# An expert mixture on one Trainium2 core: the split experts' weights in 1024-wide chunks, and one more weight buffer

## The chip, the cores and the metric

The kernel runs on one core of one Trainium2 chip. Times are device microseconds (us) of that core, from the start of an execution to its end; lower is better. TensorE (PE in the profile) does the matrix products, VectorE (DVE) and ScalarE (ACT) work on tiles, GpSimd (POOL) does little here, and SyncE (SP) issues nearly all loads from memory in one queue. Two changes are told apart when they differ by more than about half a per cent.

## The reference

Two decoder layers over 256 tokens of width 1024, all in f32. Each layer has modulation from a conditioning vector, a normalisation, a mixer (banded attention beside a state-space scan) and a channel mixer. The channel mixer of the first layer is a dense gated network; that of the second is a mixture of eight experts of hidden width 3584, of which each token uses its two best. The change is in that mixture:

```
logits = hf @ router_w
top_val, top_idx = lax.top_k(logits, 2)          # of 8 experts
gates = softmax(top_val)
# for each expert e, on the tokens that chose it:
y = (silu(xb @ w_gate[e]) * (xb @ w_up[e])) @ w_down[e]     # 1024 -> 3584 -> 1024
out[token] += gate * y
```

The weights of all eight experts are read, whatever the tokens choose: 352 MB of the 466 MB that the kernel reads.

## The kernel before

**Units and buffers.** All large weights come through one class, `Stream` (L60 to L235). It cuts them into *units* of 1 MB (128 partitions of 2048 f32) in the order in which the program uses them. `pump` (called whenever a unit is released) issues the next units on SP's queue as long as a buffer is to be had. There are eight *raw* buffers, handed out in turn, and some tiles of other stages that are *lent* to the stream when those stages are over; the trace calls them raw and slot. SP issues loads strictly in order: a load whose buffer is not yet free holds up every load behind it. The buffer that a load takes is settled when the program is built, and the loads in flight or held are at most as many as there are buffers: in the mixture the stream is 11 units ahead of its use, and 12 in its first expert.

**Two kinds of experts.** The eight experts are sorted by the number of their tokens and take places 0 to 7, which are of kinds H, L, H, L, H, L, H, L. An H expert (up to 128 tokens) works with each weight and each token value split in two parts, `hi` and `lo`: ScalarE copies half a unit to `hi` (L156) and VectorE subtracts it from the unit to get `lo` (L157), 128x1024 at a time. Five such half units fit in their pool. `mm3` (L682 to L684) then makes three matmuls for one product. A unit of an H expert is free again when both its halves have been split. An L expert (up to 64 tokens) is not split: TensorE reads the unit itself as f32 (gate and up at L1507, down at L1529), and the unit is free when its last matmul is done. An expert has 42 units: 14 each of gate, up and down.

**Chunks.** The hidden width is worked off in chunks: 512 columns wide in H experts (7 chunks, each 2 units of gate, 2 of up and 2 of down; a row of a gate or up unit is 2 KB), 1024 wide in L experts (3 such chunks and one of 512; a row is 4 KB). For each chunk the program makes gate and up, then `sg` = silu(gate) (L1636, ScalarE) times up (L1637, VectorE), and then, while the next chunk's gate and up run, turns `sg` over (`transp`, L1557 to L1559, or `transpl`, L1518 and L1552) and multiplies it with the down weights. The down units of a chunk thus stand behind the gate and up units of the next chunk, in the queue as well: the last two down units of an H expert come after the eight gate and up units of the first chunk of the L expert behind it.

**Around the experts.** Tokens are gathered by matmuls with one-hot matrices (`gather_part`, L1478, into `xh` and `xl`), for two places at a time, some of it between other matmuls (`parts`, `pend`). `combine` scales an expert's result (`yh`, L1578) and adds it to the tokens. Ahead of place 4 stands `overflow` (L1225 to L1300), a branch on the number of tokens beyond the places' capacity (L1230); with this data the number is zero and the body is not run, but each engine tests the number, and SP lets its loads land first. The body has loads of its own, `ow` (L1264, on SP's queue).

The lines that the prediction speaks of are `load` (L123) and `_split` (L156, L157) of the stream:

```
self.nc.sync.dma_start(dst, src)
...
self.last_hi = nc.scalar.activation(hi[:, o:o + w], t, AF.Copy).ins
self.last_lo = nc.vector.tensor_tensor(lo[:, o:o + w], t, hi[:, o:o + w].bitcast(F32), op=OP.subtract).ins
```

## Time and profile before

| What | Value |
|---|---|
| median of 3 runs | 1438.55 us (1433.37 to 1441.64) |
| the profiled execution | 1443.44 us, its span 1441.3 us |
| TensorE busy | 1340.4 us (93%) |
| VectorE busy | 862.2 us (60%) |
| ScalarE busy | 652.8 us (45%) |
| moved by DMA | 468.78 MB, mean 325 GB/s |
| mean granted TensorE clock | 0.970 of full speed |

The span is the time from the first to the last instruction of the profiled execution; the rest of its 1443.44 us lies around it. The mixture of experts takes from about 504 to 1427 us of the span. A mean rate over the span mixes stages with different limits, so the mixture is read from stretches of it.

### The profile page before, as it was taken

The numbers are of one execution on the slowest core, as the hardware profiler recorded it, in microseconds if no ns is written. First come the engines' busy times: TensorE is split into PE (matmuls) and PEld (weight loads), VectorE is DVE, ScalarE is ACT, GpSimd is POOL, SyncE is SP. The second block draws the span as 40 slices with busy tenths as digits, with TensorE's granted clock in tenths as the row PEclk, the third lists the DMA queues.
The fourth block names the chain that finished last, engine by engine and source line by source line (L and its number), as shares of the span: only waits on it lengthen the run. The fifth ranks groups of instructions, "written<-read, shape, count | busy, mean of one in ns | idle before, by whom it ended". The sixth has DMA issues, their size and how long they took to land. (4 is left out here: it accounts for less than half of the span.)

```text
span 1441.3 us, 20237 instructions
## 1 busy us (share of the span) xinstructions
PE 1340.4 (93%) x7642; PEld 964.4 (67%) x7642; DVE 862.2 (60%) x1299; ACT 652.8 (45%) x925; POOL 20.1 (1%) x22
## 2 busy tenths in 40 slices
PE   5999999999899899999889999969999979999985
PEld 3788699999798678864367873337885336785431
DVE  5587598777688589941068862038983116884202
ACT  3456444444456467731057742036772015773001
POOL 0020000000010000000000000000000000000000
PEclk9999999999999999999989999989999999999998
DMA  9963899999335369979999979999998999995995
GB/s 314 331 237 118 282 388 357 331 332 330 127 132 176 117 243 371 349 265 410 399 393 395 396 309 399 402 391 347 395 402 347 409 396 395 393 398 227 375 403 228
DMA packets 181478, 468.78 MB, mean 325 GB/s; under 512 B 10528, under 2 KB 39424, under 8 KB 178304
## 3 DMA queue, kind: packets, MB, share of 16 engines
q1 hardware_dynamic: 178880, 466.72, 86.3%
q8 instruction: 62, 1.02, 0.3%
q10 hardware_dynamic: 2496, 0.72, 0.2%
q14 instruction: 40, 0.33, 0.1%
HBM read 466.36 MB, written 1.05 MB: 324 GB/s over the span
## 5 line engine op out<-in xcount | busy, mean ns | idle before, releaser
L157 DVE TENSOR_TENSOR lo<-raw,hi 128x1024 fp32r<-128x1024 f32 (+1 forms) x372 | 447.0, 1226 | 138.5 <-ACT hi L156 133.9
L156 ACT ACTIVATE hi<-raw 128x1024 fp32r<-128x1024 f32 (+1 forms) x372 | 385.8, 1058 | 250.5 <-PE ps_m L683 69.3
L682 PE MATMUL ps_w<-hi,xh 128*128 128x512 f32 x448 | 183.9, 410 | 12.6 <-ACTq L1230 8.1
L683 PE MATMUL ps_w<-lo,xh 128*128 128x512 f32 x448 | 183.0, 409 | 3.4 <-DVE lo L157 3.4
L684 PE MATMUL ps_w<-hi,xh 128*128 128x512 f32 x448 | 182.0, 406 | 2.4 <-issue 2.3
L1637 DVE TENSOR_TENSOR sg<-sg,ps_w 128x512 f32<-128x512 f32 (+1 forms) x44 | 29.0, 660 | 222.0 <-PE ps_w L1507 170.6
L1507 PE MATMUL ps_w<-raw,xl 128*64 128x512 f32 (+1 forms) x688 | 143.9, 547 | 9.1 <-DMA raw<-in_moe_w_up 7.3
L682 PE MATMUL ps_m<-act_hi,hi 128*128 128x256 f32 (+1 forms) x368 | 104.6, 285 | 7.6 <-ACT hi L156 4.7
L682 PEld LDWEIGHTS ps_w<-hi,xh 128*128 128x128 f32 x448 | 87.2, 195 | 36.2 <-ACTq L1230 9.0
L1507 PEld LDWEIGHTS ps_w<-raw,xl 128*64 128x64 f32 x688 | 48.4, 136 | 85.9 <-issue 68.8
L683 PEld LDWEIGHTS ps_w<-lo,xh 128*128 128x128 f32 x448 | 87.0, 194 | 27.8 <-DVE lo L157 7.2
L683 PE MATMUL ps_m<-act_lo,hi 128*128 128x256 f32 (+1 forms) x368 | 104.3, 284 | 0.1
L684 PE MATMUL ps_m<-act_hi,lo 128*128 128x256 f32 (+1 forms) x368 | 104.0, 284 | 0.4 <-DVE lo L157 0.4
L157 DVE TENSOR_TENSOR lo<-slot,hi 128x1024 fp32r<-128x1024 f32 (+1 forms) x88 | 97.9, 1147 | 10.7 <-ACT hi L156 10.0
L684 PEld LDWEIGHTS ps_w<-hi,xh 128*128 128x128 f32 x448 | 86.8, 194 | 23.4 <-issue 3.0
L1636 ACT ACTIVATE sg<-ps_w 128x512 f32<-128x512 f32 (+1 forms) x44 | 25.3, 576 | 162.5 <-PE ps_w L1507 139.0
L156 ACT ACTIVATE hi<-slot 128x1024 fp32r<-128x1024 f32 (+1 forms) x88 | 86.3, 1000 | 25.1 <-PE ps_w L684 15.5
L1529 PE MATMUL ps_d<-raw,ht 128*64 128x512 f32 x344 | 81.0, 600 | 9.3 <-DMA raw<-in_moe_w_down 9.3
L682 PEld LDWEIGHTS ps_m<-act_hi,hi 128*128 128x128 f32 (+1 forms) x368 | 68.2, 185 | 11.5 <-ACT hi L156 5.2
L1507 PE MATMUL ps_w<-slot,xl 128*64 128x512 f32 (+1 forms) x336 | 70.9, 535 | 1.6 <-DMA slot<-in_moe_w_up 1.6
L684 PEld LDWEIGHTS ps_m<-act_hi,lo 128*128 128x128 f32 (+1 forms) x368 | 68.2, 186 | 2.8 <-issue 1.7
L683 PEld LDWEIGHTS ps_m<-act_lo,hi 128*128 128x128 f32 (+1 forms) x368 | 68.3, 186 | 0.7 <-DVE act_lo L677 0.3
(410 smaller groups left out, 2221.1 us busy)
## 6 DMA issues: line engine op xcount, KB each, us to landing
raw<-in_moe_w_down SPq DMA_DIRECT2D x87, 1024.0 KB, 14.0
raw<-in_moe_w_up SPq DMA_DIRECT2D x84, 1024.0 KB, 13.6
raw<-in_moe_w_gate SPq DMA_DIRECT2D x75, 1024.0 KB, 14.7
raw<-in_ada_w SPq DMA_DIRECT2D x40, 1024.0 KB, 6.8
slot<-in_moe_w_gate SPq DMA_DIRECT2D x46, 512.0 KB, 13.7
slot<-in_moe_w_up SPq DMA_DIRECT2D x40, 512.0 KB, 12.6
slot<-in_moe_w_down SPq DMA_DIRECT2D x30, 512.0 KB, 13.0
raw<-in_w_in SPq DMA_DIRECT2D x14, 1024.0 KB, 8.4
```

The costliest lines, as they stand in the source:

```text
L156: self.last_hi = nc.scalar.activation(hi[:, o:o + w], t, AF.Copy).ins
L157: self.last_lo = nc.vector.tensor_tensor(lo[:, o:o + w], t, hi[:, o:o + w].bitcast(F32), op=OP.subtract).ins
L682: PE.matmul(o_, s_hi, m_hi, start=start, stop=False, skip_group_check=True)
L683: PE.matmul(o_, s_hi, m_lo, start=False, stop=False, skip_group_check=True)
L684: PE.matmul(o_, s_lo, m_hi, start=False, stop=stop, skip_group_check=True)
L1507: PE.matmul(b[half * c_:half * (c_ + 1), 0:wide], xl[:, kk_, 0:half], S.col(j, o_, o_ + wide), start=(kk_ == 0), stop=(kk_ == KT - 1), ski ...
L1529: PE.matmul(y[half * c_:half * (c_ + 1), :], ht[:, ft % nm, ft // nm, :], S.col(j, t_ * D + c_ * 512, t_ * D + (c_ + 1) * 512), start=(ch ...
L1636: A.activation(sg[:, 0:wide], g[:, 0:wide], AF.Silu)
L1637: V.tensor_tensor(sg[:, 0:wide], sg[:, 0:wide], u[:, 0:wide], op=OP.mult)
```

## The change

H experts are worked off in the same chunks as L experts: three of 1024 columns and one of 512. A gate or up unit of a wide chunk then holds two row blocks of 1024 columns (a row is 4 KB) where it held four of 512, and each is multiplied into two result banks (gate: two of the pool `w`; up: one of `w` and one of `m`). `transp` and `sg` are done twice per chunk, on both halves. The gathered tokens of an L expert, `xl`, are kept only for the 64 columns in use, in the tile `masks` that held two attention masks; so the tile `act_lo`, which held `xl`, is lent to the stream as one more buffer of 1 MB for the whole mixture. The loads `ow` of the branch's body are issued on ScalarE's queue. Lines move by 2 to 14.

```diff
-    chunks = {"H": [(c0, 512) for c0 in range(0, ED, 512)], "L": [(c0, min(1024, ED - c0)) for c0 in range(0, ED, 1024)]}
+    chunks = [(c0, min(1024, ED - c0)) for c0 in range(0, ED, 1024)]
+    LAST = len(chunks) - 1
 
...
     def add_down(p, ch):
-        c0, width = chunks[kinds[p]][ch]
+        c0, width = chunks[ch]
         for r0 in range(c0, c0 + width, 2 * P):
             add_m("d", moe_w_down, p, r0, 2 * P, 0, D)
 
     first_moe = len(units)
     pend_d = None
     for p in range(NE):
-        for ch, (c0, width) in enumerate(chunks[kinds[p]]):
+        for ch, (c0, width) in enumerate(chunks):
             rows = 2048 // width * P
             for wt, tag in ((moe_w_gate, "g"), (moe_w_up, "u")):
                 for r0 in range(0, D, rows):
...
-    amask2 = const.tile([P, 2, T], BF)
-    amask4 = const.tile([P, 4, P], BF)
+    masks = act.tile([P, 2, 2 * T], BF, name="masks", tag="masks")
+    amask2 = masks[:, 0].rearrange("p (a t) -> p a t", a=2)
+    amask4 = masks[:, 1].rearrange("p (a t) -> p a t", a=4)
...
-            nc.sync.dma_start(t, w[0, bass.ds(e, 1), r0:r0 + P, c0:c0 + 512].rearrange("e p f -> p (e f)"))
+            nc.scalar.dma_start(t, w[0, bass.ds(e, 1), r0:r0 + P, c0:c0 + 512].rearrange("e p f -> p (e f)"))
...
-        xl = act.tile([P, KT, P], F32, name="xl", tag="act_lo")
+        xl = act.tile([P, KT, half], F32, name="xl", tag="masks")
 
...
+        S.lend(len(units), lambda: [act.tile([P, 2 * D], F32, name="slot", tag="act_lo")])
...
-        def proj(tag, e, b, parts=()):
+        def proj(tag, p, banks, parts=()):
             parts = list(parts)
-            for kh in range(2):
-                w = S.take((tag, e), 4)
-                for k in range(4):
-                    kk_ = kh * 4 + k
-                    if parts and k % 2 == 0:
+            nb = len(banks)
+            nk = 4 // nb
+            for kh in range(KT // nk):
+                w = S.take((tag, p), nk)
+                for k in range(nk):
+                    kk_ = kh * nk + k
+                    if parts and kk_ % 2 == 0:
                         parts.pop(0)()
-                    mm3(b, xh[:, 0, kk_, :], xh[:, 1, kk_, :], w.hi(k), w.lo(k), kk_ == 0, kk_ == KT - 1)
-                    if k % 2:
+                    for n, b in enumerate(banks):
+                        cols = (n * 512, (n + 1) * 512)
+                        mm3(b, xh[:, 0, kk_, :], xh[:, 1, kk_, :], w.hi(k, *cols), w.lo(k, *cols), kk_ == 0, kk_ == KT - 1)
+                    if nb == 2 or k % 2:
                         S.used()
             while parts:
                 parts.pop(0)()
             step_pend()
 
-        def transp(sg):
-            p_ = ps("m")
-            for j in range(4):
-                PE.transpose(p_[:, j * P:(j + 1) * P], sg[:, j * P:(j + 1) * P], ident)
-            hh = act.tile([P, 4, P], F32R, name="hh", tag="mt", bufs=2)
-            hl = act.tile([P, 4, P], F32R, name="hl", tag="pt", bufs=2)
-            pv = p_.rearrange("p (j s) -> p j s", j=4)
-            with tc.issue_after(S.last_hi):
-                A.activation(hh, pv, AF.Copy)
-            with tc.issue_after(S.last_lo):
-                V.tensor_tensor(hl, pv, hh.bitcast(F32), op=OP.subtract)
-            return hh, hl
-
-        def down(e, ch, y, hh, hl):
-            for hf in range(2):
-                w = S.take(("d", e), 2)
+        def transp(sgs):
+            out_ = []
+            for sg in sgs:
+                p_ = ps("m")
+                for j in range(4):
+                    PE.transpose(p_[:, j * P:(j + 1) * P], sg[:, j * P:(j + 1) * P], ident)
+                hh = act.tile([P, 4, P], F32R, name="hh", tag="mt", bufs=2)
+                hl = act.tile([P, 4, P], F32R, name="hl", tag="pt", bufs=2)
+                pv = p_.rearrange("p (j s) -> p j s", j=4)
+                with tc.issue_after(S.last_hi):
+                    A.activation(hh, pv, AF.Copy)
+                with tc.issue_after(S.last_lo):
+                    V.tensor_tensor(hl, pv, hh.bitcast(F32), op=OP.subtract)
+                out_.append((hh, hl))
+            return out_
+
+        def down(p, ch, y, hs):
+            for u in range(chunks[ch][1] // 256):
+                w = S.take(("d", p), 2)
                 for k in range(2):
+                    ft = u * 2 + k
+                    hh, hl = hs[ft // 4]
                     for n_ in range(2):
-                        j = hf * 2 + k
-                        mm3(y[n_], hh[:, j, :], hl[:, j, :], w.hi(k, n_ * 512, (n_ + 1) * 512),
-                            w.lo(k, n_ * 512, (n_ + 1) * 512), ch == 0 and j == 0, ch == 6 and j == 3)
+                        mm3(y[n_], hh[:, ft % 4, :], hl[:, ft % 4, :], w.hi(k, n_ * 512, (n_ + 1) * 512),
+                            w.lo(k, n_ * 512, (n_ + 1) * 512), ch == 0 and ft == 0, chunks[ch][0] + (ft + 1) * P == ED)
                     S.used()
 
...
+                nb = width // 512 if kind == "H" else 1
+                g = [ps("w") for _ in range(nb)]
                 if kind == "H":
                     proj("g", p, g, parts)
                 else:
-                    projl("g", p, width, g)
+                    projl("g", p, width, g[0])
                 parts = ()
                 if prev is not None:
                     step = flip(prev)
-                u = ps("w")
+                u = [ps(t) for t in ("w", "m")[:nb]]
                 if kind == "H":
                     proj("u", p, u)
                 else:
-                    projl("u", p, width, u)
...
-                sg = act.tile([P, 512], F32, name="sg", tag="rm", bufs=2)
-                A.activation(sg[:, 0:wide], g[:, 0:wide], AF.Silu)
-                V.tensor_tensor(sg[:, 0:wide], sg[:, 0:wide], u[:, 0:wide], op=OP.mult)
-                if ch == last and kind == "L" and p + 1 < NE:
+                sg = []
+                for g_, u_ in zip(g, u):
+                    s_ = act.tile([P, 512], F32, name="sg", tag="rm", bufs=2)
+                    A.activation(s_[:, 0:wide], g_[:, 0:wide], AF.Silu)
+                    V.tensor_tensor(s_[:, 0:wide], s_[:, 0:wide], u_[:, 0:wide], op=OP.mult)
+                    sg.append(s_)
+                if ch == LAST and kind == "L" and p + 1 < NE:
                     S.prime()
```

The order of instructions shows what this moves at three places. The first is SP's queue where expert 6 (H) ends and expert 7 (L) begins: each row is one load, a name ending in a number is the buffer's tile, and in brackets are the semaphores that it waits for (DMAHW for a landing, DVE and PE for the release of the buffer by that engine). Before:

```order
L123 DMA slot_11822<-in_moe_w_down 128x2x1024 [waits DMAHW5_49,DVE_49]
...
L123 DMA raw_11844<-in_moe_w_down 128x2x1024 [waits DMAHW6_49,DVE_49]
...
L123 DMA raw_11872<-in_moe_w_gate 128x2x1024 [waits DMAHW7_49,DVE_49]
...
L123 DMA slot_11894<-in_moe_w_gate 128x2x1024 [waits DMAHW5_49,DMAHW0_49,DVE_49]
...
L123 DMA slot_11953<-in_moe_w_gate 128x1024 [waits DMAHW1_49,PE_49]
...
L123 DMA slot_11954<-in_moe_w_gate 128x1024 [waits DMAHW2_49,PE_49]
...
L123 DMA raw_11961<-in_moe_w_gate 128x2x1024 [waits DMAHW3_49,PE_49]
```

The changed kernel, the same loads:

```order
L123 DMA raw_11793<-in_moe_w_down 128x2x1024 [waits DMAHW1_49,DVE_49]
...
L123 DMA slot_11821<-in_moe_w_down 128x2x1024 [waits DMAHW2_49,DVE_49]
...
L123 DMA raw_11843<-in_moe_w_gate 128x2x1024 [waits DMAHW3_49,DVE_49]
...
L123 DMA slot_11865<-in_moe_w_gate 128x1024 [waits DMAHW4_49,DVE_49]
...
L123 DMA slot_11866<-in_moe_w_gate 128x1024 [waits DMAHW5_49,DVE_49]
...
L123 DMA raw_11889<-in_moe_w_gate 128x2x1024 [waits DMAHW6_49,PE_49]
...
L123 DMA raw_11948<-in_moe_w_gate 128x2x1024 [waits DMAHW7_49,PE_49]
```

The first two rows are the last down units of expert 6, which stand in the queue behind the eight gate and up units of expert 7's first chunk; behind them come the gate units of its second chunk. Of these the second (two loads where its buffer is a slot of two tiles) has moved: before, it takes the slot of the first row, and waits for that unit's landing (DMAHW5) and for VectorE, which splits it; now its slot was given back by VectorE earlier, and the first load that waits for expert 7 itself (PE) is the third gate unit.

The second place is SP's queue at the branch ahead of place 4 (`COMPARE_AND_BRANCH`, L1230, now L1232). Before:

```order
L123 DMA raw_8579<-in_moe_w_down 128x2x1024 [waits DMAHW4_49,PE_49]
...
L123 DMA raw_8589<-in_moe_w_down 128x2x1024 [waits DMAHW5_49,PE_49]
...
L123 DMA raw_8602<-in_moe_w_gate 128x4x512 [waits DMAHW6_49,PE_49]
...
L123 DMA raw_8608<-in_moe_w_gate 128x4x512 [waits DMAHW7_49,PE_49]
...
L123 DMA raw_8614<-in_moe_w_up 128x4x512 [waits DMAHW0_49,PE_49]
...
L123 DMA raw_8620<-in_moe_w_up 128x4x512 [waits DMAHW1_49,DVE_49]
L1230 COMPARE_AND_BRANCH
```

The changed kernel, up to the branch, and then the first loads behind the branch's body:

```order
L123 DMA raw_8503<-in_moe_w_down 128x2x1024 [waits DMAHW4_49,PE_49]
...
L123 DMA raw_8519<-in_moe_w_gate 128x2x1024 [waits DMAHW5_49,PE_49]
...
L123 DMA raw_8529<-in_moe_w_gate 128x2x1024 [waits DMAHW6_49,PE_49]
L1232 COMPARE_AND_BRANCH
...
L123 DMA raw_8544<-in_moe_w_gate 128x2x1024 [waits DMAHW7_49,PE_49]
...
L123 DMA slot_8554<-in_moe_w_gate 128x2x1024 [waits DMAHW0_49,PE_49]
...
L123 DMA raw_8572<-in_moe_w_up 128x2x1024 [waits DMAHW1_49,PE_49]
```

The branch has moved up by eight loads: it stood behind the last up unit of expert 4's second chunk, and it stands now behind that expert's second gate unit.

The third is TensorE where expert 4 (H) ends and expert 5 (L) begins; `oh` and `htok` are the one-hot matrix and the tokens of the gather, `ps_w` is a bank of gate or up. Before:

```order
L683 MATMUL ps_a<-lo,hh 128x512
L684 MATMUL ps_a<-hi,hl 128x512
L1478 MATMUL ps_m<-oh,htok_h 128x256 [waits PE_49]
L1478 MATMUL ps_m<-oh,htok_h 128x256 x3
L1478 MATMUL ps_m<-oh,htok_l 128x256 [waits PE_49]
L1478 MATMUL ps_m<-oh,htok_l 128x256 x3
L1478 MATMUL ps_m<-oh,htok_h 128x256 [waits PE_49]
L1478 MATMUL ps_m<-oh,htok_h 128x256 x3
L1478 MATMUL ps_m<-oh,htok_l 128x256 [waits PE_49,Activation_49]
L1478 MATMUL ps_m<-oh,htok_l 128x256 x3
L1507 MATMUL ps_w<-raw,xl 64x512 [waits DMAHW0_49,DVE_49]
```

The changed kernel, at the first matmuls of this gather:

```order
L684 MATMUL ps_w<-hi,xh 128x512 [waits Activation_49]
L1480 MATMUL ps_m<-oh,htok_l 128x256 [waits DVE_49,PE_49]
L1480 MATMUL ps_m<-oh,htok_l 128x256 x3
L1480 MATMUL ps_m<-oh,htok_h 128x256 [waits DVE_49,PE_49]
L1480 MATMUL ps_m<-oh,htok_h 128x256 x3
L685 MATMUL ps_w<-lo,xh 128x512 [waits DVE_49]
L686 MATMUL ps_w<-hi,xh 128x512
L684 MATMUL ps_w<-hi,xh 128x512
```

The gather stood in one piece between the last down matmuls of expert 4 and the first gate matmuls of expert 5 (L1507); it now stands between matmuls of expert 4's last gate and up.

## Rows read from the trace of the kernel before

**Rows 1.** The page: busy time by engine, and GB/s in 40 slices.

```profile
PE 1340.4 (93%) x7642; PEld 964.4 (67%) x7642; DVE 862.2 (60%) x1299; ACT 652.8 (45%) x925; POOL 20.1 (1%) x22
...
GB/s 314 331 237 118 282 388 357 331 332 330 127 132 176 117 243 371 349 265 410 399 393 395 396 309 399 402 391 347 395 402 347 409 396 395 393 398 227 375 403 228
```

**Rows 2.** Stretches inside an L expert, an H expert, an H expert's gate units.

```profile
core 0: us, PE busy (x) PEld busy (x) DVE busy (x) ACT busy (x) POOL busy (x), PEclk, DMA share, GB/s
880.00:920.00 40.00, 39.05 (x186) 15.63 (x187) 5.54 (x11) 3.66 (x6) 0.00 (x0) 1.00 1.03 409
1020.00:1040.00 20.00, 20.00 (x92) 16.23 (x91) 18.22 (x17) 16.10 (x18) 0.00 (x0) 1.00 1.04 392
785.00:787.50 2.50, 2.50 (x13) 2.01 (x12) 2.50 (x3) 1.55 (x2) 0.00 (x0) 1.00 1.05 387
```

**Rows 3.** The same view where experts pass from H to L, and the branch.

```profile
610.00:620.00 10.00, 10.00 (x47) 8.13 (x46) 8.97 (x9) 7.67 (x9) 0.00 (x0) 1.00 0.75 249
620.00:630.00 10.00, 10.00 (x56) 8.05 (x55) 3.27 (x8) 2.23 (x7) 0.00 (x0) 1.00 0.49 193
630.00:640.00 10.00, 10.00 (x51) 4.02 (x51) 6.68 (x13) 5.37 (x8) 0.00 (x0) 1.00 0.54 186
...
850.00:860.00 10.00, 10.00 (x54) 6.97 (x54) 5.15 (x12) 1.33 (x5) 0.00 (x0) 1.00 0.70 269
860.00:870.00 10.00, 10.00 (x46) 3.27 (x44) 0.00 (x0) 3.83 (x6) 0.00 (x0) 1.00 0.51 175
970.00:980.00 10.00, 10.00 (x44) 6.02 (x43) 6.85 (x7) 5.67 (x7) 0.00 (x0) 1.00 0.65 230
...
1090.00:1100.00 10.00, 10.00 (x50) 4.07 (x50) 1.66 (x5) 2.48 (x4) 0.00 (x0) 1.00 0.57 181
...
1310.00:1320.00 10.00, 10.00 (x59) 7.15 (x59) 3.08 (x6) 1.15 (x3) 0.00 (x0) 1.00 0.74 294
1320.00:1330.00 10.00, 10.00 (x50) 3.39 (x48) 0.00 (x0) 4.87 (x6) 0.00 (x0) 1.00 0.00 0
1330.00:1340.00 10.00, 7.44 (x22) 4.53 (x19) 5.82 (x6) 0.00 (x0) 0.00 (x0) 0.72 0.43 149
```

**Rows 4.** SP's timeline: start and length of issuing a few loads, waiting included.

```profile
620.52 14.79 SPq L123 DMA_DIRECT2D raw<-in_moe_w_gate  x3
...
852.73 11.46 SPq L123 DMA_DIRECT2D raw<-in_moe_w_gate  x2
...
1079.64 18.25 SPq L123 DMA_DIRECT2D raw<-in_moe_w_gate  x3
...
1311.77 0.37 SPq L123 DMA_DIRECT2D raw<-in_moe_w_gate  x1
1334.52 1.55 SPq L123 DMA_DIRECT2D slot<-in_moe_w_gate  x3
```

**Rows 5.** TensorE's timeline at the three later passages.

```profile
858.00 3.65 PE L1507 MATMUL ps_w<-slot,xl 128*64 128x512 f32 x14
...
861.84 1.94 PE L1507 MATMUL ps_w<-raw,xl 128*64 128x512 f32 x8
...
1084.05 0.63 PE L1478 MATMUL ps_m<-oh,htok_h 128*128 128x256 f32 x4
...
1316.72 1.94 PE L1507 MATMUL ps_w<-slot,xl 128*64 128x512 f32 x8
```

**Rows 6.** VectorE's timeline where expert 7 begins; in brackets idle before, releaser.

```profile
1331.53 0.69 DVE L1637 TENSOR_TENSOR sg<-sg,ps_w 128x512 f32<-128x512 f32 x1 [14.53 <-PE ps_w L1507]
1332.13 2.35 DVE L157 TENSOR_TENSOR lo<-slot,hi 128x1024 fp32r<-128x1024 f32 x2
1334.41 0.68 DVE L1559 TENSOR_TENSOR hl<-ps_m,hh 128x512 fp32r<-128x512 f32 x1
```

**Rows 7.** The branch on TensorE's queue: count, ns minimum, median, maximum.

```profile
L1230 PEldq COMPARE_BRANCH  x1: 6286/6286/6286, 948.6 to 948.6; - x1
```

**Rows 8.** ScalarE's timeline at expert 4's first landing.

```profile
950.66 2.00 ACT L156 ACTIVATE hi<-raw 128x1024 fp32r<-128x1024 f32 x2 [15.94 <-DMA raw<-in_moe_w_gate]
```

**Rows 9.** The chain that ended last: start, length, what, line.

```profile
1406.67 18.06 DMA raw<-in_moe_w_down
```

More of the change, by code (lines that the diff above doesn't have):

```diff
@@ L1482, in gather_part @@
                 if kinds[p] == "L":
-                    A.activation(xl[:, ks], banks[0][:, :, q], AF.Copy)
-                    V.tensor_tensor(xl[:, ks], banks[1][:, :, q], xl[:, ks], op=OP.add)
+                    A.activation(xl[:, ks], banks[0][:, :, q, 0:half], AF.Copy)
+                    V.tensor_tensor(xl[:, ks], banks[1][:, :, q, 0:half], xl[:, ks], op=OP.add)
                 else:
@@ L1506, in projl @@
                         o_ = k * width + c_ * wide
-                        PE.matmul(b[half * c_:half * (c_ + 1), 0:wide], xl[:, kk_, 0:half],
+                        PE.matmul(b[half * c_:half * (c_ + 1), 0:wide], xl[:, kk_, :],
                                   S.col(j, o_, o_ + wide), start=(kk_ == 0), stop=(kk_ == KT - 1), skip_group_check=True)
@@ L1521, in downl @@
         def downl(p, ch, y, ht):
-            c0, width = chunks["L"][ch]
+            c0, width = chunks[ch]
             nm = width // 2 // P
@@ L1599, in flip @@
             if kinds[p] == "H":
-                hh, hl = transp(sg_)
-                return lambda y: down(p, ch, y, hh, hl)
-            ht = transpl(sg_, chunks["L"][ch][1])
+                hs = transp(sg_)
+                return lambda y: down(p, ch, y, hs)
+            ht = transpl(sg_[0], chunks[ch][1])
             return lambda y: downl(p, ch, y[0], ht)
@@ L1607, in moe @@
             kind = kinds[p]
-            last = len(chunks[kind]) - 1
             if p == 4:
@@ L1613, in moe @@
             parts = gather((0,), oh0) if p == 0 else ()
-            for ch, (c0, width) in enumerate(chunks[kind]):
-                final = (p, ch) == (NE - 1, last)
+            for ch, (c0, width) in enumerate(chunks):
+                final = (p, ch) == (NE - 1, LAST)
                 if final:
                     fin = prefinish(p, inf)
-                g = ps("w")
+                nb = width // 512 if kind == "H" else 1
+                g = [ps("w") for _ in range(nb)]
                 if kind == "H":
@@ L1629, in moe @@
                 else:
-                    projl("u", p, width, u)
-                ahead = together[p // 2 + 1] if ch == last and p % 2 == 0 else None
+                    projl("u", p, width, u[0])
+                ahead = together[p // 2 + 1] if ch == LAST and p % 2 == 0 else None
                 if ahead:
@@ L1644, in moe @@
                     step(prev[3])
-                    if prev[2] == len(chunks[kinds[prev[1]]]) - 1:
+                    if prev[2] == LAST:
                         pend.extend(combine(prev[1], prev[3]))
```

## Prediction

> **What bounds the kernel now.** The page first: TensorE is busy for 1340.4 us of the span, VectorE for 862.2, and the row of GB/s shows two kinds of stage, one at 390 to 410 and one far below [rows 1]. A TensorE that is busy 93% of the time looks like the bound. In the mixture (504 to 1427 us) it is only half of it, and the windows show why. Inside an L expert the loads run at 409 GB/s with the DMA share at 1.03, while VectorE works 5.54 of 40 us; inside an H expert TensorE works 20.00 of 20 us, VectorE 18.22, and the loads still run at 392 [rows 2]. An expert has 42 units of 1.0486 MB. At 409 GB/s a unit takes 2.56 us, so 42 take 108 us. Expert 4, an H, takes TensorE from its first landing at 950.66 [rows 8] to the end of its down matmuls at 1084.05 [rows 5], 133 us, so during an H expert the stream gains on its user until it stands the whole look-ahead ahead, and during the L expert behind it TensorE eats that lead and then waits for landings. As long as the queue always finds a free buffer, the loads run through, and loads set the time of the mixture: the chain that ended last ends with a landing of a down unit [rows 9]. So what can be won is the time in which DMA stands still though units are left to load.
>
> The windows at the four passages from H to L show exactly that [rows 3]. Each rate against 409 gives lost time, 10 us times (1 minus the rate over 409). Passage 0 to 1: 3.9, 5.3 and 5.5, together **14.6 us**. Passage 2 to 3: 3.4 and 5.7, **9.1**. The branch: **4.4** in 970 to 980. Passage 4 to 5: **5.6**. Passage 6 to 7: 2.8, 10.0 and 6.4, **19.2**. All together 52.9 us. Why DMA stands there, SP's timeline tells: three loads take 14.79 us to issue from 620.52, two take 11.46 from 852.73, three take 18.25 from 1079.64, and between 1311.77 and 1334.52 none is issued [rows 4]. At the head of the queue stands a load of the L expert's second chunk whose buffer is not free, and nothing can pass it.
>
> **The change part by part.**
>
> *The extra buffer and the new order of buffers (loss or gain at each passage).* A load more ahead of the blocked one gives DMA 2.56 us of work in the stall; a buffer that comes free earlier ends the stall earlier. What each passage gets back is the sum of the two, up to what it loses now. I followed which unit's buffer the blocked load takes, from the order of instructions.
>
> - *0 to 1.* The blocked load takes the buffer of expert 1's first gate unit, before and after, but two more loads stand ahead of it: 2 x 2.56 = **5.1 us** of the 14.6. If one of the two is itself late, 2.6.
> - *2 to 3.* The block was on the buffer of expert 3's third unit, whose matmuls end at 861.84 + 1.94 = 863.78; now it is on the second unit's, and its matmuls end at 858.00 + 3.65 = 861.65 [rows 5]. One more load and 2.1 us: **4.7 us** of the 9.1. Below: the load alone, 2.6; above: if earlier gathering helps too, 7.
> - *4 to 5.* One more load (2.56), and the gather that stood alone ahead of expert 5 (it begins at 1084.05, eight groups of four matmuls at 0.63 us each, about 5.0 [rows 5]) now lies between earlier matmuls, so expert 5 releases its first unit that much sooner. 7.6 is more than the 5.6 lost: the stall is gone, **5.6 us**. And because no stall follows, a faster stream in expert 4 counts here: see the rows of 4 KB below, **3.6 us**. Together 9.2; below, the load alone, 2.6.
> - *6 to 7.* The load that is blocked until 1334.5 takes the buffer of expert 6's last down units. VectorE splits these only after the product `sg` of expert 7's first chunk, at 1331.53, for which it sat idle 14.53 us, and the split lasts from 1332.13 to 1334.5 [rows 6]. Now that load has a slot that was given back earlier, and the first blocked load waits for expert 7's first gate unit, whose matmuls end at 1316.72 + 1.94 = 1318.66 [rows 5]: 2.56 + (1334.5 - 1318.6) = 18.5 us. Take **18.5** of the 19.2; below, 2.6, if the block stays with VectorE.
>
> *Rows of 4 KB for 2 KB.* The gate units of an H expert, in rows of 2 KB, ran at 387 GB/s [rows 2], 2.71 us for a unit, against 2.56 at 409: 0.15 us for each of the 24 units of three wide chunks, 3.6 us an H expert. In front of a passage with a stall it buys nothing, for the queue only runs into the stall earlier; it is therefore counted once, at 4 to 5. The Trainium skill ("DMA: Bandwidth & Descriptors", Specifications) puts the smallest transfer for line rate at 512 B, so by it 2 KB rows would be as fast as 4 KB rows and the sum would be 3.6 us smaller; the trace's 387 against 409 speaks against it, though weakly, since VectorE and TensorE were busiest in that stretch.
>
> *Two banks, two `transp`, two `sg` in an H chunk.* Matmuls, splits and products stay as many; they come in larger groups. A bunch has a price if TensorE waits for VectorE at the chunk's end. In the only place where the profile shows such a bunch, VectorE takes 2.35 us for two `lo` and 0.68 for one `hl` [rows 6]. The four H experts have 16 chunk ends now, where they had 28. I set the price at nothing: VectorE works 18.22 of 20 us in an H expert [rows 2], so it has 9% of slack, and a wait of TensorE in an H expert moves the passage, not the loads, until the look-ahead is full. The bounds are a gain of 12 x 0.68 = 8 us and the loss of the last rival below.
>
> *The branch.* It moves up eight loads in SP's queue, and SP drains its loads there as before: 4.4 us lost, before and after. ScalarE now has the body's loads `ow` in its code. TensorE's test took 6.29 us [rows 7]; if ScalarE's took as long, it would end in ScalarE's idle time of 15.94 us before expert 4's first landing [rows 8]. The cover gone, it costs 6.3 at most. The Trainium skill ("Runtime: NRT & Kernel Launch", Instruction fetch mechanics) says that a branch out of the prefetched code must fetch its target first; by that the longer body would cost ScalarE a fetch, and the sum would be 6.3 smaller if nothing covered it.
>
> *Masks and the half-width `xl`:* no engine does more than before, and the masks are last read long before `xl` is written: nothing.
>
> **Sum.** 5.1 + 4.7 + 9.2 + 18.5 = 37.5 us. The profiled execution would go from 1443.44 to 1405.9; it lay 4.89 us above the median of the runs, so the median would go from 1438.55 to **1401 us**.
>
> **The rivals.** Half a per cent, 7.2 us, is about what a measurement of this kernel tells from no change.
>
> *A. As summed.* With 2 to 3 to its upper bound, and 6 to 7 giving all 19.2 and half of the 9.5 left at 0 to 1: some 10 more, 1391; if all 52.9 that DMA loses were given back, 1385. With the branch's 6.3 and the 3.6 of the rows lost: 1411. Chance 0.62.
>
> *B. Passage 6 to 7 stays blocked.* The slots come free by VectorE, which in that stretch waits for TensorE; a split in another order would hold a load as long as before. Then 18.5 becomes 2.6, and the time 1417; with 4 to 5 at its lower end as well, 1424. Against it: the order shows no load of that stretch that takes the buffer of expert 6's last units. Chance 0.20.
>
> *C. Nothing.* The loads are not the bound over two experts: TensorE's busy 20.00 of 20 us in H is, and a passage passed sooner is waited for later. By this each passage gives its lower bound less what the bunching takes: 2.6 x 4 = 10.4 gained and some 8 to 16 lost at 16 chunk ends of 0.5 to 1 us, 1436 to 1444. For it: TensorE is busy 93% [rows 1]. Against it: 14.53 us of VectorE's and 10 us of DMA's idleness at once in 1320 to 1330. Chance 0.10.
>
> *D. Slower.* At the end of every wide chunk TensorE waits for VectorE: two up banks (one of them in the pool `m`, which `transp` and gather use too) must be multiplied out before the banks come free, behind the two `lo` and one `hl` of 2.35 + 0.68 = 3.0 us [rows 6]. At 16 chunk ends that is 48.5 us, against 37.5 won: 1449.5. It decides (slower by over 7.2) from (37.5 + 7.2)/16 = 2.8 us a chunk end, if all of it falls on the path. Against it: TensorE has the other banks to go on with, and a wait of 2.8 us in each chunk would show as a busy share near 0.9, where the H stretch now shows 1.0. Chance 0.08.
>
> **How the numbers follow.** The time is that of A. The range takes A from 1385 on, and B with its 1424 and a few us of A's own loss beside it, to 1430: 0.82 less the edges, about 0.8. Faster by over 7.2: A and B, 0.82. Within 7.2: C mostly, 0.10. Slower: D, 0.08.
>
> **What would show it.** Right: no stretch of 10 us without loads at passage 6 to 7, and the passage's loss under 2 us; expert 2's first landing earlier by 5 us, expert 4's by 10, expert 6's by 19; 0 to 1 still losing about 9 us, the branch 4 to 5; gate units of H experts at 405 or more. Wrong: TensorE idle before the first down or gate matmuls of each chunk with VectorE as releaser (D), a load of passage 6 to 7 issued only after `sg` of expert 7 (B), or landings earlier by as much as forecast with an end that is not (C). The forecast fails most easily if the stall goes elsewhere: a later load of an H expert that takes a buffer of a unit split late, which the buffers at the passages alone don't show.

## The result, and the profile after

The changed kernel takes 1401.95 us (median of 4 runs, 1400.82 to 1404.46), the kernel before 1440.1 (4 runs, 1433.37 to 1442.63): a ratio of 0.9745, 95% interval 0.9707 to 0.9782. The forecast was 1401 us, with 1385 to 1430 as the range.

The profiled execution of the changed kernel took 1400.82 us, its span 1398.7. The page, busy time by engine and GB/s in 40 slices (35 us each), against [rows 1]:

```profile
PE 1318.8 (94%) x7641; PEld 954.9 (68%) x7642; DVE 857.2 (61%) x1299; ACT 647.6 (46%) x925; POOL 20.1 (1%) x22
...
GB/s 313 346 249 100 275 389 366 323 350 335 167 126 147 196 148 343 365 310 362 402 409 409 404 407 383 407 353 410 409 402 385 406 402 409 409 402 402 402 402 182
```

From the twentieth slice to the last but one, three of twenty are under 400 (383, 353, 385). VectorE and ScalarE have as many instructions as before (1299 and 925); what has gone is time without loads. The windows at the passages from H to L and at the branch, against [rows 3]; the columns are the same:

```profile
610.00:620.00 10.00, 10.00 (x45) 8.09 (x44) 9.42 (x11) 7.42 (x9) 0.00 (x0) 1.00 0.80 290
620.00:630.00 10.00, 10.00 (x58) 7.37 (x57) 4.63 (x9) 4.58 (x11) 0.00 (x0) 1.00 0.68 240
630.00:640.00 10.00, 10.00 (x49) 3.88 (x50) 3.43 (x10) 1.42 (x3) 0.00 (x0) 1.00 0.73 245
840.00:850.00 10.00, 10.00 (x57) 6.35 (x58) 4.12 (x11) 1.13 (x3) 0.00 (x0) 1.00 0.87 345
850.00:860.00 10.00, 10.00 (x49) 3.19 (x45) 0.00 (x0) 4.86 (x6) 0.00 (x0) 1.00 1.00 382
...
930.00:940.00 10.00, 4.33 (x18) 2.02 (x15) 2.86 (x4) 3.87 (x5) 0.00 (x0) 0.80 0.65 230
1070.00:1080.00 10.00, 10.00 (x48) 3.29 (x46) 0.27 (x2) 2.22 (x3) 0.00 (x0) 1.00 0.93 325
1290.00:1300.00 10.00, 10.00 (x50) 3.49 (x48) 0.00 (x0) 4.86 (x6) 0.00 (x0) 1.00 0.98 366
1300.00:1310.00 10.00, 7.44 (x31) 4.10 (x28) 5.83 (x6) 0.00 (x0) 0.00 (x0) 1.00 1.01 401
```

Worked out as in the prediction (10 us times 1 minus the rate over 409), the loads lose now 2.9 + 4.1 + 4.0 = 11.0 us at 0 to 1 (14.6 before), 1.6 + 0.7 = 2.3 at 2 to 3 (9.1), 4.4 at the branch (4.4), 2.1 + 0.3 at 4 to 5 (5.6; the 0.3 is the next stretch, at 397), and 1.1 + 0.2 at 6 to 7 (19.2). That is 21.4 of 52.9: **31.5 us** less. SP's timeline at 6 to 7, against [rows 4], shows no gap of 20 us any more; the longest from one start to the next is 8:

```profile
1280.46 0.37 SPq L123 DMA_DIRECT2D raw<-in_moe_w_gate  x1
1281.60 1.48 SPq L123 DMA_DIRECT2D slot<-in_moe_w_gate  x2
1289.85 2.10 SPq L123 DMA_DIRECT2D raw<-in_moe_w_gate  x2
1293.29 4.54 SPq L123 DMA_DIRECT2D raw<-in_moe_w_up  x2
```

VectorE does what it did in [rows 6]: it is idle for 14.54 us ahead of expert 7's first `sg`, and only then makes the two `lo`. Two loads still wait for these splits, one for 4.2 us and one for 1.6 (the third line has SP's waits from 1300 to 1310 us: in total, times, longest). They are loads of down units, no longer the second gate unit, and so many loads stand ahead of them that the rate stays at 401 GB/s and over:

```profile
1302.68 0.69 DVE L1650 TENSOR_TENSOR sg<-sg,ps_w 128x512 f32<-128x512 f32 x1 [14.54 <-PE ps_w L1510]
1303.29 2.35 DVE L157 TENSOR_TENSOR lo<-raw,hi 128x1024 fp32r<-128x1024 f32 x2
...
SPq L123 <- DVE lo L157: 5.8, 2, 4.2
```

The rest of the gain is the rate between the passages. Windows inside experts 2, 4 and 6, first before, then after:

```profile
720.00:840.00 120.00, 115.68 (x491) 88.90 (x490) 93.91 (x94) 80.41 (x87) 0.00 (x0) 0.96 1.04 396
990.00:1070.00 80.00, 80.00 (x356) 64.23 (x355) 73.52 (x71) 61.01 (x64) 0.00 (x0) 1.00 1.04 396
1190.00:1300.00 110.00, 108.30 (x464) 83.16 (x464) 88.07 (x89) 74.11 (x81) 0.00 (x0) 0.97 1.04 396
```

```profile
720.00:840.00 120.00, 118.34 (x534) 93.06 (x533) 99.33 (x103) 83.65 (x96) 0.00 (x0) 1.00 1.03 407
950.00:1060.00 110.00, 107.67 (x484) 83.53 (x483) 90.47 (x93) 77.16 (x88) 0.00 (x0) 1.00 1.03 407
1160.00:1280.00 120.00, 117.20 (x519) 90.30 (x518) 99.94 (x100) 85.98 (x94) 0.00 (x0) 1.00 1.03 407
```

396 against 407 GB/s is 120 x 11/407 = 3.2 us in an expert, if each has 120 us of such loads; in three experts that is **9.7 us**. Together 41.2. The trace has 924.5 us from the first gate matmul of expert 0 to the first matmul of the finish before (503.7 to 1428.2) and 883.7 after (501.6 to 1385.3): 40.8 us. The two agree better than the counting is good: it leaves out some 3 us that the changed kernel's loads lose near their end (368 and 315 GB/s from 1360 to 1380). The medians differ by 38.2 and the two profiled executions by 42.6: that of the kernel before took 1443.44 us at a mean granted clock of 0.970, where runs of the same kernel at 0.978 and more took 1434 to 1439, so some us of the 41.2 may be that execution's and not the change's.

By first gate matmul, the stages of the eight experts took (us):

| | H0 | L1 | H2 | L3 | H4 | L5 | H6 | L7 |
|---|---|---|---|---|---|---|---|---|
| before | 123.3 | 94.9 | 134.1 | 101.2 | 128.9 | 96.4 | 134.2 | 111.5 |
| after | 124.0 | 89.8 | 130.0 | 93.1 | 131.1 | 87.3 | 131.0 | 97.4 |

The L experts became shorter by 5 to 14 us each; the H experts, whose code was rewritten, changed by 1 to 4.

### The profile page after: what moved, and what is told of

The parts are those of the page before. It is cut to its first block, busy times and chain, and to the rows that moved or that the text cites. A ratio compares the mean times of both kernels' runs of the same rounds, so it can differ in the third digit from the quotient of the medians.

```text
span 1398.7 us, 20224 instructions
## 1 busy us (share of the span) xinstructions
PE 1318.8 (94%) x7641; PEld 954.9 (68%) x7642; DVE 857.2 (61%) x1299; ACT 647.6 (46%) x925; POOL 20.1 (1%) x22
## 5 line engine op out<-in xcount | busy, mean ns | idle before, releaser
L157 DVE TENSOR_TENSOR lo<-raw,hi 128x1024 fp32r<-128x1024 f32 (+1 forms) x328 | 393.3, 1227 | 93.0 <-ACT hi L156 90.2
L156 ACT ACTIVATE hi<-raw 128x1024 fp32r<-128x1024 f32 (+1 forms) x328 | 341.2, 1059 | 206.8 <-PE ps_m L685 69.0
L157 DVE TENSOR_TENSOR lo<-slot,hi 128x1024 fp32r<-128x1024 f32 (+1 forms) x132 | 149.6, 1171 | 29.5 <-ACT hi L156 29.5
L685 PE MATMUL ps_w<-lo,xh 128*128 128x512 f32 x352 | 142.6, 405 | 4.2 <-DVE lo L157 4.2
L156 ACT ACTIVATE hi<-slot 128x1024 fp32r<-128x1024 f32 (+1 forms) x132 | 130.1, 1018 | 28.5 <-DMA slot<-in_moe_w_gate 10.6
L686 PE MATMUL ps_w<-hi,xh 128*128 128x512 f32 x352 | 140.6, 401 | 0.2 <-DVE xh L1489 0.2
L684 PE MATMUL ps_w<-hi,xh 128*128 128x512 f32 x352 | 132.9, 407 | 6.7 <-ACT hi L156 5.4
L685 PEld LDWEIGHTS ps_w<-lo,xh 128*128 128x128 f32 x352 | 67.7, 192 | 24.1 <-DVE lo L157 7.3
L684 PEld LDWEIGHTS ps_w<-hi,xh 128*128 128x128 f32 x352 | 67.1, 192 | 24.5 <-ACT hi L156 8.1
L686 PEld LDWEIGHTS ps_w<-hi,xh 128*128 128x128 f32 x352 | 67.2, 191 | 16.1 <-DVE xh L1489 0.7
L1532 PE MATMUL ps_d<-raw,ht 128*64 128x512 f32 x296 | 68.7, 598 | 1.5 <-DMA raw<-in_moe_w_down 1.5
L1604 DVE SCALAR_TENSOR_TENSOR xT<-ps_m,modT,xT 128x256 f32<-128x256 f32 x56 | 24.6, 479 | 53.7 <-PE ps_m L1601 53.6
## 6 DMA issues: line engine op xcount, KB each, us to landing
raw<-in_moe_w_up SPq DMA_DIRECT2D x77, 1024.0 KB, 12.1
slot<-in_moe_w_gate SPq DMA_DIRECT2D x40, 512.0 KB, 13.7
```

What stands on the lines that cost most here:

```text
L684: PE.matmul(o_, s_hi, m_hi, start=start, stop=False, skip_group_check=True)
L685: PE.matmul(o_, s_hi, m_lo, start=False, stop=False, skip_group_check=True)
L686: PE.matmul(o_, s_lo, m_hi, start=False, stop=stop, skip_group_check=True)
L1532: PE.matmul(y[half * c_:half * (c_ + 1), :], ht[:, ft % nm, ft // nm, :], S.col(j, t_ * D + c_ * 512, t_ * D + (c_ + 1) * 512), start=(ch ...
L1604: V.scalar_tensor_tensor(xT[:, m_, :], p_[:, k * T:(k + 1) * T], mod(1, 5)[:, m_:m_ + 1], xT[:, m_, :], op0=OP.mult, op1=OP.add)
```

## The experiments

Ratios are to the kernel before, run on the same chip; the changed kernel's own is 0.9745. The median of the kernel before lies between 1435 and 1440 us from chip to chip, so two experiments on different chips are compared by their ratios; 0.001 is 1.4 us.

**Chunks without the buffer, and the buffer without the chunks.** The first run takes one line out of the changed kernel:

```diff
-        S.lend(len(units), lambda: [act.tile([P, 2 * D], F32, name="slot", tag="act_lo")])
```

> The changed kernel without the extra buffer (the tile act_lo is not lent): wide chunks alone. Theory of the prediction (what counts is which buffer the blocked load takes): the load that lost passage 6 to 7 its 19 us no longer takes the buffer of expert 6's last down units, so that passage gives 14 to 17 us back even without the buffer; 0 to 1 stays at 14.6 us lost, since its blocked load stands where it stood; 4 to 5 gives about 5; the rows of 4 KB give the rate of 409 GB/s in the H experts. In all 20 to 30 us: 1410 to 1420 us. Rival (the number of buffers makes the gain): 1430 to 1440 us, with a stretch of 10 us without loads at 6 to 7.

The second adds that line, the tile `masks` and the half-width `xl` to the kernel before, whose H chunks stay 512 wide.

> The kernel before with the extra buffer alone: masks in a tile of their own that then holds the half-width tokens, act_lo lent to the stream, chunks of H experts 512 wide as before. Theory of the prediction: passages 0 to 1 and 2 to 3 give 5 and 4.7 us, 6 to 7 gives 16 to 18, since the blocked load there now waits for TensorE on expert 7's first gate unit; the rows of 2 KB stay at 387 to 395 GB/s; at 4 to 5 a load takes a buffer that is split late, so that passage gives nothing or loses some us. In all 20 to 28 us: 1412 to 1420. Rival (the order of work in wide chunks makes the gain): within 8 us of before, 1432 or more.

They took 1411.18 us (0.9821, 0.9789 to 0.9853) and 1412.12 us (0.9830, 0.9800 to 0.9860): each alone gives about two thirds of the gain, as the theory of the blocked load's buffer had it, and both rivals fall. The stretches at 6 to 7 show that either of them does away with most of the stall or all of it. Chunks alone:

```profile
1290.00:1300.00 10.00, 10.00 (x58) 7.12 (x58) 3.41 (x7) 1.11 (x3) 0.00 (x0) 1.00 0.79 300
1300.00:1310.00 10.00, 10.00 (x50) 3.42 (x48) 0.00 (x0) 4.86 (x6) 0.00 (x0) 1.00 0.94 331
```

Buffer alone, and its passage 4 to 5:

```profile
1070.00:1080.00 10.00, 10.00 (x58) 5.03 (x57) 2.09 (x8) 1.46 (x5) 0.00 (x0) 1.00 0.78 313
1080.00:1090.00 10.00, 10.00 (x46) 4.57 (x45) 5.92 (x6) 4.52 (x6) 0.00 (x0) 1.00 0.67 217
1290.00:1300.00 10.00, 10.00 (x60) 7.62 (x60) 3.47 (x7) 0.83 (x3) 0.00 (x0) 1.00 1.02 408
1300.00:1310.00 10.00, 10.00 (x50) 3.41 (x48) 0.00 (x0) 4.86 (x6) 0.00 (x0) 1.00 1.03 410
```

With chunks alone 6 to 7 loses 4.6 us where the changed kernel loses 1.3; one load less ahead of the blocked one (2.56) is most of the difference. With the buffer alone it loses nothing. But with the buffer alone 4 to 5 loses 7.0, more than the 5.6 of before: there the new order makes a load wait 11.9 us for VectorE's split of a unit of expert 4, so the trap of 6 to 7 has moved to 4 to 5. SP's waits from 1070 to 1084 us:

```profile
SPq L123 <- DVE lo L157: 12.4, 2, 11.9
```

From 720 to 840 us the chunks alone ran at 406 GB/s, the buffer alone at 397: the rate belongs to the chunks.

**The order of splits in the kernel before.** In an L expert's first chunk VectorE is made to split first:

```diff
-                V.tensor_tensor(sg[:, 0:wide], sg[:, 0:wide], u[:, 0:wide], op=OP.mult)
+                if ch == 0 and kind == "L":
+                    with tc.issue_after(S.last_lo):
+                        V.tensor_tensor(sg[:, 0:wide], sg[:, 0:wide], u[:, 0:wide], op=OP.mult)
+                else:
+                    V.tensor_tensor(sg[:, 0:wide], sg[:, 0:wide], u[:, 0:wide], op=OP.mult)
```

> The kernel before with one edit: in the first chunk of an L expert VectorE does the product sg after the last lo that was ordered, so it splits the previous H expert's down unit before it waits for TensorE (two places move on VectorE, passages 2 to 3 and 6 to 7). Theory: the buffer is given back some 12 to 15 us sooner at 6 to 7, SP issues there, and the 19.2 us lost fall to 4 to 8; time 1424 to 1429 us. Rival (the load waits for something else there, or what is won is lost later): within 3 us of before.

1431.52 us, 0.9960 (0.9941 to 0.9978): faster, by 3 to 8 us, but 1424 to 1429 us were expected. SP's and ScalarE's timelines say why:

```profile
1326.19 1.55 SPq L123 DMA_DIRECT2D slot<-in_moe_w_gate  x3
```

```profile
1322.23 0.60 ACT L1636 ACTIVATE sg<-ps_w 128x512 f32<-128x512 f32 x1 [7.48 <-PE ps_w L1507]
1322.73 2.00 ACT L156 ACTIVATE hi<-slot 128x1024 fp32r<-128x1024 f32 x2
```

The load went out at 1326.2 instead of 1334.5. What held it then was ScalarE: silu, for which it sat idle 7.48 us, stood ahead of the copy to `hi`, from which VectorE makes `lo`. My expectation had left out the other engine of the split. The next run puts silu behind the last `hi` in the same way.

> The kernel before with the edit on VectorE, and the same on ScalarE: in an L expert's first chunk silu is done after the last hi that was ordered. With VectorE alone the blocked load was issued at 1326.2 instead of 1334.5, because ScalarE still did silu, for which it waits for TensorE, ahead of the copy to hi. Theory: now the load is issued once its unit has landed and is split, near 1316 to 1319, and 6 to 7 loses 3 to 5 us of 19.2; another 5 to 8 us faster than with VectorE alone, 1424 to 1427. Rival (the landing itself or the next load, which waits for TensorE, holds the queue): within 2 us of the run with VectorE alone.

1422.98 us, 0.9901 (0.9880 to 0.9923): a little better than expected. The load went out at 1314.1 now; one stretch of 10 us still falls short of the full rate, and the next, which had no loads at all before, is at the full rate:

```profile
1314.06 1.55 SPq L123 DMA_DIRECT2D slot<-in_moe_w_gate  x3
```

```profile
1310.00:1320.00 10.00, 10.00 (x53) 4.11 (x54) 3.74 (x6) 3.80 (x6) 0.00 (x0) 1.00 0.90 337
1320.00:1330.00 10.00, 10.00 (x45) 5.25 (x42) 2.96 (x3) 1.56 (x2) 0.00 (x0) 1.00 1.02 412
```

6 to 7 loses 1.8 us where it lost 19.2, and expert 7 took 96.9 us where it took 111.5. Two instructions set in another order, with buffers and chunks as before, give 14 us in the whole kernel, and 17.4 of the 19.2 us at 6 to 7 hung on this chain.

**The same order in the changed kernel.** First VectorE's part alone:

> The changed kernel with the same one edit on VectorE (three places: 2 to 3, 4 to 5, 6 to 7). Theory: no load waits for those splits any more, so the loads are not moved; what goes is TensorE's wait of about 2.5 us at the first down matmuls of the previous H expert, and this counts only behind 6 to 7, where TensorE sets the end: 0 to 3 us faster. Rival (all of the wait is on the path): 6 to 8 us faster.

1397.66 us, 0.9728 (0.9704 to 0.9752). Then ScalarE's part too:

> The changed kernel with both edits of order (in an L expert's first chunk VectorE does sg and ScalarE does silu after the splits of the previous H expert's down units). Theory: no load waits for these splits in the changed kernel, so only TensorE's short waits at the first down matmuls go, which the edit on VectorE alone has taken: 0 to 2 us faster than with that one, 1395 to 1399. Rival (silu later delays what follows on TensorE): 1 to 4 us slower than with VectorE alone.

1397.96 us, 0.9718 (0.9695 to 0.9741). By the ratios they are 2 and 4 us faster than the changed kernel, in the direction expected, but the intervals overlap its own; that they are faster is likely and not settled. The expectations said that no load waits for these splits any more, and that is not so: two do, as shown above. They stand far enough back in the queue that loads do not run out meanwhile, so the order of the splits is worth little here.

**Rows of 2 KB.** In the changed kernel each gate and up unit that goes to a whole buffer is loaded by two transfers, each of 512 columns, and in the control by two of one row block each (the lines around these choose the units):

```diff
...
+                    for h in range(2):
+                        self.nc.sync.dma_start(dst[:, :, h * 512:(h + 1) * 512], src[:, :, h * 512:(h + 1) * 512])
...
```

```diff
...
+                    for h in range(2):
+                        self.nc.sync.dma_start(dst[:, h:h + 1], src[:, h:h + 1])
...
```

> The changed kernel in which each gate and up unit of a wide chunk that goes to a whole 1 MB buffer is loaded by two transfers of 512 columns each, so with rows of 2 KB, in H and L experts alike. Theory (rows of 2 KB run at 387, rows of 4 KB at 409 GB/s): such stretches fall to 385 to 395 GB/s, and with some 140 such units at 0.15 us the time rises by up to 20 us; since TensorE now sets part of the time, 8 to 20 us over the changed kernel, 1410 to 1422. Rival (the 387 of before came from busy engines, and row length changes nothing): as the control with two transfers of 4 KB rows.

> The control: the same units loaded by two transfers each, but one for each row block, so rows stay 4 KB. Theory: the number of transfers costs nothing that shows, 409 GB/s stays, within 3 us of the changed kernel, 1399 to 1405. Rival (twice the transfers cost by themselves): slower by 8 us or more, as much as the run with rows of 2 KB.

1413.29 us (0.9833, 0.9813 to 0.9852) against 1401.18 us (0.9744, 0.9721 to 0.9767): 12 us for the length of a row, none for the number of transfers. From 720 to 840 us, rows of 2 KB, then the control:

```profile
720.00:840.00 120.00, 118.34 (x536) 93.04 (x535) 99.78 (x102) 83.91 (x96) 0.00 (x0) 1.00 1.04 396
```

```profile
720.00:840.00 120.00, 118.28 (x532) 91.20 (x531) 99.66 (x103) 82.55 (x95) 0.00 (x0) 1.00 1.03 407
```

VectorE and TensorE are as busy in the one as in the other, and 396 and 407 are just the rates of before and after. So it was the rows.

**The branch's loads** back on SP's queue (`nc.scalar` to `nc.sync` in the branch's body):

> The changed kernel with the loads of the branch's body back on SP's queue. The body is not run with this data. Theory: ScalarE's longer code is skipped in its idle time ahead of expert 4's first landing, so nothing changes: within 3 us of 1402. Rival (ScalarE's skip of the body costs up to 6.3 us on the path, which this gives back): 1395 to 1398, and expert 4's first matmul some 5 us earlier behind the branch.

1399.3 us, 0.9737 (0.9717 to 0.9757): no difference that can be told from the changed kernel. ScalarE does pay for the longer code that it skips. Its rows at the branch, in the changed kernel and then in this one, give start times in the middle:

```profile
L1232 ACTq COMPARE_BRANCH  x1: 54/54/54, 922.7 to 922.7; - x1
...
L1232 ACTq EVENT_SEMAPHORE  x1: 17/17/17, 928.1 to 928.1; - x1
```

```profile
L1232 ACTq COMPARE_BRANCH  x1: 54/54/54, 935.1 to 935.1; - x1
L1232 ACTq EVENT_SEMAPHORE  x1: 17/17/17, 935.7 to 935.7; - x1
```

The next row comes 5.4 us behind the test with the loads on ScalarE's queue, and 0.6 us without them. In the changed kernel this falls into 13.63 us in which ScalarE sits idle for TensorE, and so costs nothing. In this kernel SP met the branch at 939.4 us, in the changed one at 917.9, where it then stood until 935.9 for its landings; the branch costs 4 to 5 us of loads in either (213 GB/s in the lowest stretch of 10 us of this kernel, 230 in the changed one).

**What bounds the changed kernel.** Expert 6 leaves out the last of `mm3`'s three matmuls, the one with the tokens' remainder (`short` is true in expert 6 alone):

```diff
...
-        PE.matmul(o_, s_hi, m_lo, start=False, stop=False, skip_group_check=True)
-        PE.matmul(o_, s_lo, m_hi, start=False, stop=stop, skip_group_check=True)
+        PE.matmul(o_, s_hi, m_lo, start=False, stop=stop and short, skip_group_check=True)
+        if not short:
+            PE.matmul(o_, s_lo, m_hi, start=False, stop=stop, skip_group_check=True)
```

> The changed kernel in which expert 6 leaves out the third of mm3's matmuls (token remainder times weight), so its output lacks that small term and TensorE has 168 of 504 x 3 / 3, that is a third, fewer matmuls there, some 38 us; the loads are as before. It asks what bounds the changed kernel behind expert 5. Theory: TensorE and the loads are close together now, so DMA takes over as the bound as soon as TensorE is faster: expert 7 ends 5 to 12 us sooner, 1390 to 1397. Rival 1 (TensorE alone is the bound): 30 us or more faster, under 1372. Rival 2 (the loads are the bound still): within 3 us of the changed kernel.

1396.94 us, 0.9711 (0.9683 to 0.9739): 5 us faster than the changed kernel, at the lower edge of what the theory gave and far from the 30 of rival 1. By the intervals it is only likely that this is more than nothing, so rival 2 (within 3 us) is not ruled out. Expert 6 took 114.8 us where it took 131.0, expert 7 then 110.1 where it took 97.4. Two stretches show the engines that came up next:

```profile
1200.00:1240.00 40.00, 37.21 (x138) 21.92 (x137) 39.47 (x42) 33.95 (x36) 0.00 (x0) 1.00 1.03 409
...
1320.00:1350.00 30.00, 25.78 (x120) 8.54 (x120) 0.69 (x1) 0.60 (x1) 0.00 (x0) 1.00 1.03 408
```

In expert 6 VectorE works 39.47 of 40 us, and through expert 7 the loads run at 408 while TensorE has pauses. In the changed kernel the chain that ends last goes through TensorE at the end, where in the kernel before it went through landings [rows 9]; with fewer matmuls in expert 6 it goes through landings again. A piece of that chain (start, length, what) in the changed kernel, then in this run:

```profile
1373.29 10.47 PE ps_d L1532 x48
```

```profile
1360.34 18.23 DMA slot<-in_moe_w_down
```

So TensorE and the loads are within some 5 us of each other in the changed kernel.

**The gather ahead of the down matmuls.** In the kernel with both orders this moves the gather of the next two places:

```diff
+                if ahead:
+                    for f in gather(ahead, oh):
+                        f()
                 if prev is not None:
                     step(prev[3])
...
-                if ahead:
-                    for f in gather(ahead, oh):
-                        f()
```

> The changed kernel with both edits of order, and the gather of the next two places put ahead of the H expert's down matmuls of its last chunk but one. Passage 0 to 1 is where most is lost still (11 us of loads), since the blocked load waits for expert 1's first gate unit and the gather's eight groups stand ahead of that unit on TensorE. Theory: the unit is done some 5 us sooner, the loss at 0 to 1 falls to 5 to 7, and since the loads set the time from 640 on, the whole is 3 to 6 us faster than with both edits alone, 1391 to 1395. Rival (the split of expert 0's down unit holds the queue there, not expert 1's first unit): within 2 us, 1396 to 1400.

1398.72 us, 0.9745 (0.9718 to 0.9772; its six runs lie between 1394 and 1406, and the profiled one is the fastest): nothing gained, as the rival has it. Stretches of its passage 0 to 1 gave 110, 323 and 380 GB/s, 10.1 us lost where the kernel with both orders loses 11.1. SP's timelines, the kernel with both orders and then this one:

```profile
617.72 0.39 SPq L123 DMA_DIRECT2D raw<-in_moe_w_gate  x1
620.52 8.23 SPq L123 DMA_DIRECT2D slot<-in_moe_w_gate  x3
633.12 0.38 SPq L123 DMA_DIRECT2D raw<-in_moe_w_gate  x1
```

```profile
619.02 0.39 SPq L123 DMA_DIRECT2D raw<-in_moe_w_gate  x1
621.82 3.17 SPq L123 DMA_DIRECT2D slot<-in_moe_w_gate  x3
628.32 0.38 SPq L123 DMA_DIRECT2D raw<-in_moe_w_gate  x1
```

The load that waits for expert 1's first unit did go out 4.8 us sooner. But the loads ahead of it wait for splits of expert 0's down units, and the first of these came later, behind the gather. From 615 us to that load's issue SP waits 13.7 us for `lo` (5.9 the longest) and 4.1 for expert 1 in the kernel with both orders, and 13.9 (10.1 the longest) and 3.1 in this one. So the rival was right in the main: most of the waiting at 0 to 1 is for splits. Expert 0's stage grew from 124.2 to 127.5 us, expert 1's shrank from 88.6 to 85.1. The stall was moved ahead, not removed.

## Why the prediction was right

The time (1401.95 for 1401) and the mechanism were right. The forecast's gain was 37.5 us and the medians give 38.2, but the terms, as the windows measure them, were off by -0.6, -1.5, +2.1, -2.4 and +6.1 us in the order below. These partly cancel, and that the time was met within 1 us is in part luck.

- *6 to 7* (18.5 us forecast): 19.2 lost before, 1.3 after, so 17.9. The cause is shown three ways: by the order of splits alone, by the chunks alone and by the buffer alone. What the prediction had not seen is that ScalarE's silu stood in the chain too. And its argument against rival B, that no load of that stretch takes the buffers of expert 6's last units, was too strong: two loads of down units do, without harm, because they stand further back.
- *0 to 1* (5.1): 3.6 by the windows, and 5.1 by expert 1's stage. Two loads more stand ahead of the blocked one, as read from the order, but the second waits 5.9 us for a split of an expert 0 unit itself, the lower case that the prediction named.
- *2 to 3* (4.7, up to 7): 6.8. The blocked load was held for 6.4 us where it was held for 10.5, so 4.1 us less and not 2.1; why was not tried.
- *4 to 5* (5.6, the stall gone): 3.2. The earlier gather did what was forecast: the blocked load was held for 7.1 us where it was held for 12.1. But it went out at 1071.6, only 2.3 us before the last load ahead of it landed, and the loads behind it followed one by one as expert 5 released its units, so 2.4 us are still lost. Why the loads had run down that far was not tried; a faster stream in expert 4 would do it, by the prediction's own rule for a passage that blocks.
- *Rows of 4 KB*: the mechanism was right and the size wrong. I counted 3.6 us once, because a stall behind each other passage would eat it. It is about 3.2 us in each of three experts, 9.7, since the change left only 1.3 to 2.4 us of stall at the passages behind them to eat it. As I read it, a passage that blocks swallows a faster stream only as long as it blocks; what that is worth at each passage was not measured.
- *The Trainium skill* ("DMA: Bandwidth & Descriptors", Specifications) puts line rate at 512 B and more. The two runs with rows of 2 and 4 KB disagree: 396 against 407 GB/s, with as many transfers and engines as busy.
- *Two banks, two `transp`, no price*: H stages changed by +0.7, -4.1, +2.2 and -3.2 us; TensorE's waits for VectorE's `lo` at the down matmuls sum to 5.9 us in the whole changed kernel (3.1 before). Rival D needed 2.8 at each of 16 chunk ends, 45 us. The price need not be nothing: the mean granted clock in experts 2, 4 and 6 was 0.96, 0.97 and 0.96 of full speed before and is 0.99, 0.98 and 1.00 after. With each stage multiplied by its clock, the four H stages grew by some 6 us together, an estimate.
- *The branch*: 4.4 lost before and after, as forecast. ScalarE's longer code takes 5.4 us, near the 6.3 that was allowed for, and it is covered.
- *Rival C* (TensorE bounds, nothing gained) was wrong for the kernel before; the changed kernel has come near it.
- *The signs*: the stretch without loads at 6 to 7 is gone, and the rate in H experts is 407. The first gate matmuls of experts 2, 4 and 6 came 6.5, 18.7 and 25.6 us earlier, 2.1 of it from ahead of the mixture, where landings 5, 10 and 19 us earlier were named: more was won around experts 2 and 3 than I had.
- *A slip in the sum*: what rival A adds for its lower end (2.3 at 2 to 3, 0.7 at 6 to 7, half of 9.5 at 0 to 1) is 7.8 us and not 10, so 1393 and not 1391; the range does not hang on it.

## What to carry to other kernels

A queue that issues in order stops at the first load whose buffer is not free. What decides is which buffer that load takes and how many loads stand ahead of it, more than how many buffers there are: look up at each change of stage whose release the head of the queue waits for, and follow that release back through every engine that makes it. Two engines' instruction order alone was worth 14 us here, one buffer alone 24, and a buffer can move the trap to another passage. And a gain that is hidden by a stall comes back when the stall goes, so terms that are set to nothing behind a stall are to be counted again without it.

## What the runs showed of the hardware

Transfers into 128 partitions with rows of 2 KB ran at 396 GB/s and with rows of 4 KB at 407, in stretches with two thirds of such units, with engines equally busy and twice the number of transfers without effect (396, 397, 396 in three kernels with rows of 2 KB; 407, 406, 407 in three with 4 KB).

A branch around a body whose loads are issued by ScalarE kept ScalarE from its next row for 5.4 us; with those loads on SP's queue it was 0.6 us (0.5 in the kernel before). TensorE's own test at that branch took 4.5 to 6.3 us in three kernels.
